# The dense attention's keys and values move into seven-product pairs, and its conditioning is summed in wider pieces

## The chip, the cores and the metric

The kernel runs on one core of one Trainium2 chip. The metric is the device time of one execution, in microseconds (us), as the median of several runs. One more execution was recorded by the hardware profiler; all views of the profile below come from that one.

## The reference

One inference step of a trunk with two layers, for 512 latent tokens and 128 context tokens (640 columns in all, width 2048). Every layer does the same: RMS norm of x with a scale and a shift that come from a conditioning vector, one input projection whose columns feed two mixers and their gates, one output projection, and a gated residual. The conditioning of a layer is `silu(cond) @ ada_w[layer] + ada_b[layer]`, 6144 columns for each of two vectors.

The second ("odd") layer is the one that the change touches:

```
cq, ck, cv, cg, dq, dk, dv, dg = split_cols(h @ w_in, ODD_SPLIT)   # 1024,1024,1024,1024,1024,256,256,1024
o_c = rms_norm(o1 - lam * o2, c_on) * (1 - lam_init)               # mixer C: two softmax maps for each of 4 heads
y_d = merge_heads(attend(q_d, dk_all, dv_all)) * silu(dg)          # mixer D: 8 query heads, 2 key/value heads
x   = x + gate * (concatenate([y_c, y_d]) @ w_out)
```

Mixer D is dense attention: queries and keys are normed and turned by a rotary table, the latent tokens attend to 256 cached context tokens and all 512 latents, the context tokens only to themselves. Its two key heads and two value heads are 128 columns each, so each is one tile of the projection. The new keys and values of the context tokens are outputs as well.

## The kernel before

All activations lie transposed: 16 tiles of 128 channels by 640 tokens. A projection **tile** is 128 output channels: 16 blocks of weights, each held as a high and a low part (`split`, L295, one ACT copy and one DVE subtraction, L296 and L297), times the activations, held in the same way. Three products (high x high, high x low, low x high) and two halves of 320 tokens make 96 matmuls of 128x320 in `proj_q` (L324, L331 to L333). A **quarter** of a tile is four blocks, 24 matmuls.

Where several tiles need only be projected, two are taken together as a **pair** in `run_pairs` (L523): a two by two scheme of seven products of half the size instead of eight. Each product is 8 blocks x 3 = 24 matmuls of 128x320 (L616 to L618); the combined weights are summed on DVE (L555 to L567), the combined activations (`forms`, L1137) were made once. After each of the seven products (M1, M5, M6, M2, M7, M3, M4) `after` copies or adds its result (L588 copies that of M1).

The second layer has three stages.

- **The front** (`project`, called at L1671 with `run_pairs` behind it) projects 14 of the 16 gate tiles and the eight value tiles of mixer C, 22 tiles: the first `N_FRONT = 6` singly, the other 16 as eight pairs. `front_begin` (L1652) chooses what becomes of each tile. A gate (`gate_out`) is stored to a scratch tensor in DRAM; a value (`value_out`, `value_rows`) is copied to SBUF, transposed to token rows by PE, copied by ACT and stored to the scratch `vdram` and, for the context tokens, to the output, both on POOL's DMA queue.
- **The odd stage** (`run_tiles` with the list `jobs`, L1689 to L1710) projects the remaining tiles singly and works the attention in between. Its 28 jobs are, for each half of mixer D, `dq0 dq1 dk dv dq2 dq3`, and then, for each head of mixer C, `cq cq ck ck`; two late gates follow. The function of a finished tile (`q_gen` L727, `k_gen` L660, `v_gen` L774) is a generator, put on the list `prep`.
- **The output projection** (`project_out`, called at the end).

What sets the order: the code issues a quarter of a tile and then calls `slot` (L371). A slot takes every generator of `prep` one step on, takes the attention list `attn` on by `steps` steps (1.0 by default; `brisk` gives 1.1 from job 13 on and 1.5 for the last two jobs), and takes the fill on by `rate` steps (`FILL1 = 1.3`, from the ninth slot on). All of `prep` is drained before the next tile's generator begins. Attention generators (`pair_gen` L858 for two heads of mixer D, `diff_gen` for mixer C) make about two steps for each block of 128 queries, one for each score. `k_gen` and `v_gen` call `drain(attn)` before they write the tiles that the attention reads, so that a second key or value first forces out all attention that is still waiting; `q_gen` does so while as many attentions wait as there are sets of query tiles (two). A score takes the only PSUM buffer of the name `S` (L826), and gives it back when the exponential (L800) has read it. From this list the compiler makes each engine's own order, which need not be the code's.

A weight quarter is loaded on SP's queue up to five quarters ahead into four buffers (`RAW_AHEAD`, `load_raw`, L309) and split three ahead (`SPLIT_AHEAD`).

The fill is `ada_on_dve` (L191): the last four 512-column blocks of the layer's conditioning. Each block is summed over 16 row blocks on DVE, for two conditioning vectors, in two parts of 256 columns; `scalar_tensor_tensor` (L218) multiplies by the vector's element and adds. The weights come on SP's queue (L206, tile `adaw`, three buffers) one step ahead. A copy from the last weight split (`mark`) keeps a block from starting before its place.

## Time and profile before

| | us |
|---|---|
| median of 3 runs | 2280.9 |
| lowest and highest run | 2277.78 and 2281.18 |
| the profiled execution | 2276.21 |
| its span, from the first to the last instruction | 2274.3 |

The granted TensorE clock was 0.997 of full speed on average. In the views, PE is the matmul engine, PEld its weight loading, DVE, ACT and POOL the three others, and SP the engine that issues most loads. A name such as `pa<-h,wh` gives the tile written and the tiles read; L331 is a line of the kernel before. Matmuls overlap each other, so their mean duration (some 310 ns) is longer than the distance from one to the next, and idle time of PE counts only what no matmul covers.

### The profile page before, as it was taken

The page shows a single profiled execution, that of the slowest core. Times are in us where ns is not written, and L with a number is a line of the kernel's source. Part 1 is how long each engine was busy: PE and PEld are TensorE (multiplying, and loading weights), DVE is VectorE, ACT ScalarE, POOL GpSimd, SP SyncE. Part 2 cuts the span into 40 slices and gives each one's busy share as a digit, 9 for nine tenths or more (in the row PEclk, how much of TensorE's full clock was granted, in tenths as well). Part 3 has the DMA queues.
Part 4 walks back from the last instruction along what each step waited for, and adds up shares of the span by engine and source line. Part 5 has one row for each costly group of instructions (what it writes and reads, how often), then busy time and mean ns, then how long its engine had stood idle before and what let it go on. Part 6 is the DMA issues. An engine that isn't in the chain of part 4 may idle for free.

```text
span 2274.3 us, 41403 instructions
## 1 busy us (share of the span) xinstructions
PE 2237.6 (98%) x15760; PEld 2155.6 (95%) x15760; DVE 1680.4 (74%) x3133; ACT 1113.0 (49%) x2293; POOL 207.9 (9%) x305
## 2 busy tenths in 40 slices
PE   8999999999999999999999999999999999999999
PEld 5889999999799999999999999999999999999999
DVE  5659889987857778887876754857758788677665
ACT  4336554544334445444744455566665455554343
POOL 2220000000000000000200000010010211211010
PEclk9999999999999999999999999999999999999999
DMA  9984556564833326643763334423324234237541
GB/s 358 344 292 145 175 172 202 168 186 148 261 102 99 91 91 225 212 141 112 250 213 109 114 109 135 132 70 96 100 75 147 89 107 126 89 119 241 152 135 49
DMA packets 387400, 351.45 MB, mean 155 GB/s; under 512 B 17906, under 2 KB 341968, under 8 KB 386688
## 3 DMA queue, kind: packets, MB, share of 16 engines
q1 hardware_dynamic: 373360, 298.15, 42.9%
q0 software_dynamic: 12976, 48.41, 5.8%
q8 instruction: 124, 2.03, 0.4%
q10 hardware_dynamic: 864, 2.23, 0.3%
q14 instruction: 76, 0.62, 0.1%
HBM read 305.86 MB, written 42.86 MB: 153 GB/s over the span
## 4 chain that ended last, share of the span: by engine, by line
PE 84%; DVE 5%; DMA 4%; ACT 3%; issue 2%; POOL 1%; SPq 0%; DVEq 0%; ACTq 0%; POOLq 0%
PE pq L617 10%; PE pq L618 10%; PE pq L616 10%; PE pa L331 7%; PE pb L331 6%; PE pb L332 6%; PE pa L332 6%; PE pb L333 6%; PE pa L333 6%; PE T L819 2%; PE S L831 1%; DMA adaw<-in_ada_w 1%; PE S L833 1%; PE S L832 1%; PE T L646 1%
## 5 line engine op out<-in xcount | busy, mean ns | idle before, releaser
L296 ACT ACTIVATE wh<-raw 128x512 fp32r<-128x512 f32 (+1 forms) x400 | 241.2, 604 | 412.3 <-PE pb L332 289.4
L331 PE MATMUL pa<-h,wh 128*128 128x320 f32 x1216 | 389.4, 320 | 0.5 <-DVE sum L420 0.5
L332 PE MATMUL pa<-h,wh 128*128 128x320 f32 x1216 | 378.5, 311 | 0.9 <-DVE h L297 0.9
L331 PE MATMUL pb<-h,wh 128*128 128x320 f32 x1216 | 378.2, 312 | 0.9 <-ACT h L296 0.9
L333 PE MATMUL pb<-h,wl 128*128 128x320 f32 x1216 | 377.8, 311 | 0.0
L332 PE MATMUL pb<-h,wh 128*128 128x320 f32 x1216 | 377.7, 311 | 0.0
L333 PE MATMUL pa<-h,wl 128*128 128x320 f32 x1216 | 377.3, 310 | 0.0
L297 DVE TENSOR_TENSOR wl<-raw,wh 128x512 fp32r<-128x512 f32 (+1 forms) x400 | 262.1, 656 | 151.1 <-ACT wh L296 138.2
L616 PE MATMUL pq<-h,wh 128*128 128x320 f32 x896 | 277.2, 309 | 0.0
L618 PE MATMUL pq<-h,wl 128*128 128x320 f32 x896 | 276.9, 309 | 0.0
L617 PE MATMUL pq<-h,wh 128*128 128x320 f32 x896 | 276.8, 309 | 0.0
L331 PEld LDWEIGHTS pa<-h,wh 128*128 128x128 f32 x1216 | 228.8, 188 | 16.1 <-issue 11.0
L332 PEld LDWEIGHTS pa<-h,wh 128*128 128x128 f32 x1216 | 229.0, 188 | 7.3 <-issue 6.2
L331 PEld LDWEIGHTS pb<-h,wh 128*128 128x128 f32 x1216 | 229.4, 189 | 2.9 <-issue 1.2
L332 PEld LDWEIGHTS pb<-h,wh 128*128 128x128 f32 x1216 | 229.3, 189 | 1.3 <-issue 1.2
L333 PEld LDWEIGHTS pa<-h,wl 128*128 128x128 f32 x1216 | 228.4, 188 | 2.1 <-issue 2.1
L333 PEld LDWEIGHTS pb<-h,wl 128*128 128x128 f32 x1216 | 229.3, 189 | 0.4 <-issue 0.4
L616 PE MATMUL pq<-T,wh 128*128 128x320 f32 x672 | 208.0, 309 | 0.0
L617 PE MATMUL pq<-T,wh 128*128 128x320 f32 x672 | 207.6, 309 | 0.0
L618 PE MATMUL pq<-T,wl 128*128 128x320 f32 x672 | 207.3, 308 | 0.0
L258 DVE SCALAR_TENSOR_TENSOR acc<-adaw,sT,acc 128x1024 f32<-128x1024 f32 x150 | 189.5, 1280 | 0.0
L296 ACT ACTIVATE wh<-sx 128x512 fp32r<-128x512 f32 x168 | 105.6, 633 | 147.5 <-PE pq L617 101.0
(379 smaller groups left out, 4634.5 us busy)
## 6 DMA issues: line engine op xcount, KB each, us to landing
adaw<-in_ada_w SPq DMA_DIRECT2D x80, 512.0 KB, 3.9
raw<-in_od_w_in SPq DMA_DIRECT2D x160, 256.0 KB, 2.9
raw<-in_ev_w_in SPq DMA_DIRECT2D x130, 256.0 KB, 3.4
ada<-in_ada_w SPq DMA_DIRECT2D x11, 2048.0 KB, 13.8
adaw<-in_ada_w SPq DMA_DIRECT2D x128, 128.0 KB, 2.2
w<-in_ev_w_in SPq DMA_DIRECT2D x27, 512.0 KB, 3.7
w<-in_od_w_in SPq DMA_DIRECT2D x24, 512.0 KB, 3.8
adah<-in_ada_w SPq DMA_DIRECT2D x20, 512.0 KB, 9.5
```

The costliest lines, as they stand in the source:

```text
L258: V.scalar_tensor_tensor(out=acc[c], in0=w, scalar=sT[:, kt, c:c + 1], in1=acc[c], op0=ALU.mult, op1=ALU.add)
L296: A.activation(hi, x, AF.Copy)
L297: V.tensor_sub(lo, x, hi)
L331: PE.matmul(ps, wh[:, i, :], hi[:, sl], start=(j == js[0] if alone else (pos == 0 and j == 0)), stop=False)
L332: PE.matmul(ps, wh[:, i, :], lo[:, sl], start=False, stop=False)
L333: PE.matmul(ps, wl[:, i, :], hi[:, sl], start=False, stop=(j == js[1] - 1 if alone else (pos == 3 and j == 3)))
L616: PE.matmul(ps, wh[:, j, :], hi, start=(first and h == 0 and j == 0), stop=False, skip_group_check=True)
L617: PE.matmul(ps, wh[:, j, :], lo, start=False, stop=False, skip_group_check=True)
L618: PE.matmul(ps, wl[:, j, :], hi, start=False, stop=(final and h == 1 and j == 3), skip_group_check=True)
L646: PE.transpose(t[:, i * P:(i + 1) * P], src(b), ident)
L819: PE.transpose(t[:, i * P:(i + 1) * P], p, ident)
L831: PE.matmul(d, q[0][:, bs], k[0][:, ks], start=True, stop=False)
```

## The change

The two key tiles and the two value tiles of mixer D leave the list of jobs and join the front's list, as two more pairs between the gates and the values of mixer C. The front has 26 tiles and ten pairs, the odd stage 24 jobs and the two late gates.

A key is copied to SBUF by `key_out` and stored to a new scratch tensor `kdram`. At the start of the odd stage `keys_first` loads both, and `k_gen` works them one after the other, two steps in each slot (`in_twos`). A value goes the way of mixer C's values, with two more places of `vdram`; its rows come back in `with_values`, a first step ahead of the attention of each half's first pair of heads, which also splits them and the cached values.

The fill sums 512 columns at a time: half as many loads, twice as large, two buffers for three. `FILL1` becomes 0.85. `brisk` gives 1.5 attention steps a slot for jobs 2 to 9 and 1.1 from job 10 on. Three small things make room in SBUF: two unused results (`junk`) are written as bf16, and `le` shares the tile of `ls`.

```diff
-FILL1 = 1.3
+FILL1 = 0.85
...
+    def ada_on_dve(blocks):
...
+            acc = [ap.tile([P, 512], F32, tag=f"acc{c}", name=f"acc{c}", bufs=1) for c in range(2)]
+            for c in range(2):
+                V.tensor_copy(acc[c][:, 0:1], mark[0])
+            def fetch(kt):
+                w = ap.tile([P, 512], F32, tag="adaw", name="adaw", bufs=2)
+                nc.sync.dma_start(w, I["ada_w"][l, kt * P:(kt + 1) * P, cb * 512:(cb + 1) * 512])
+                return w
+            nxt = fetch(0)
+            for kt in range(KT):
+                w, nxt = nxt, (fetch(kt + 1) if kt + 1 < KT else None)
                 for c in range(2):
...
+                        V.scalar_tensor_tensor(out=acc[c], in0=w, scalar=sT[:, kt, c:c + 1], in1=acc[c],
                                                op0=ALU.mult, op1=ALU.add)
                 yield
...
-        x = stage(ap, pp)
+        if isinstance(pp, tuple):
+            x = stage(ap, pp)
+        else:
+            x = ap.tile([P, NT], F32, tag="stg", name="kx", bufs=2)
+            nc.sync.dma_start(x, pp)
...
+    def with_values(values, ap, width, k, *rest):
+        rows_, src = values
+        raw = ap.tile([P, 5, P], F32, tag="ctxv", name="vrow", bufs=1)
+        ctx_ = ap.tile([P, 2, P], F32, tag="ctxk", name="vctx", bufs=1)
+        nc.sync.dma_start(raw.rearrange("p b f -> p (b f)"), rows_)
+        nc.sync.dma_start(ctx_, src.rearrange("(c p) d -> p c d", p=P))
+        yield
+        hi, lo = st["v"] = tuple(ap.tile([P, 7, P], F32R, tag=t, name=t) for t in ("vh", "vl"))
+        split(hi[:, 2:7, :], lo[:, 2:7, :], raw)
+        split(hi[:, 0:2, :], lo[:, 0:2, :], ctx_)
+        yield from pair_gen(ap, width, k, st["v"], *rest)
...
-        nc.gpsimd.dma_start(O["new_c_v"][0, 0, n // 2][:, n % 2 * P:(n % 2 + 1) * P], r[:, 4, :])
+        nc.gpsimd.dma_start(O["new_c_v"][0, 0, n // 2][:, n % 2 * P:(n % 2 + 1) * P] if n < 8
+                            else O["new_d_v"][0, 0, n - 8], r[:, 4, :])
...
+    def key_out(j):
+        x = xr_tile("kx")
+        def put(t, sl, src):
+            A.copy(x[:, sl], src)
+            if (j, "k") in half_done:
+                nc.gpsimd.dma_start(kdram[j], x)
+            half_done.add((j, "k"))
+        return put
...
-            + [OD["cv"] + i * P for i in range(8)], N_FRONT, h1_maker,
+            + [OD[n] + i * P for n, m in (("dk", 2), ("dv", 2), ("cv", 8)) for i in range(m)], N_FRONT, h1_maker,
...
-        then = pair_then(768, f"k{kv}", 8 + h, False, gated)
+        then = pair_then(768, f"k{kv}", 8 + h, False, gated,
+                         (vdram[8 + kv], I["cache_d_v"][0, 0, kv]) if n % 2 == 0 else None)
         jobs.append((OD["dq"] + h * P, q_job("q0", "d_q_norm")))
-        jobs.append((OD["dq"] + (h + 1) * P, q_job("q1", "d_q_norm", then if n % 2 else None)))
-        if n % 2 == 0:
-            jobs.append((OD["dk"] + kv * P, k_job(f"k{kv}", I["cache_d_k"][0, 0, kv], "d_k_norm", O["new_d_k"][0, 0, kv])))
-            jobs.append((OD["dv"] + kv * P, v_job(I["cache_d_v"][0, 0, kv], O["new_d_v"][0, 0, kv], then)))
+        jobs.append((OD["dq"] + (h + 1) * P, q_job("q1", "d_q_norm", then)))
+    def keys_first():
+        for kv in range(2):
+            yield from k_job(f"k{kv}", I["cache_d_k"][0, 0, kv], "d_k_norm", O["new_d_k"][0, 0, kv])(kdram[kv])
+    def in_twos(g):
+        while next(g, DONE) is not DONE and next(g, DONE) is not DONE:
+            yield
+    prep.append(in_twos(keys_first()))
...
-    brisk.update((i, 1.1) for i in range(13, len(jobs)))
+    brisk.update((i, 1.5 if i < 10 else 1.1) for i in range(2, len(jobs)))
```

More of the change, by code (lines that the diff above doesn't have):

```diff
@@ L675, in k_gen @@
         kg = ap.tile([P, 5, P], F32, tag="rp", name="kg", bufs=3)
-        junk = ap.tile([P, P * st["sets"]], F32, tag="junk", name="junk", bufs=1)[:, 0:P]
+        junk = ap.tile([P, P * st["sets"]], BF16, tag="junk", name="junk", bufs=1)[:, 0:P]
         for sample in (True, False):
@@ L932, in trunk_kernel @@
     fill0b = ada_beside([(1, 2), (1, 3)])
-    fill1 = ada_on_dve([(1, cb) for cb in range(8, 12)], ("acc0", "acc1", "adaw", "adaw", "adaw", "adaw"), 2,
-                       lambda: mark[-1])
+    fill1 = ada_on_dve([(1, cb) for cb in range(8, 12)])
     ydram = [dram.tile([P, NT], F32, name=f"yd{k}") for k in range(KT)]
     x0dram = [dram.tile([P, 4 * NT + 1], F32, name=f"x0d{g}") for g in range(4)]
+    kdram = [dram.tile([P, NT], F32, name=f"kd{k}") for k in range(2)]
     xdram, hdram, gdram, vdram = ([dram.tile([P, NT], F32, name=f"{n}{k}") for k in range(KT)]
@@ L1057, in gate_job, with pair_then @@
         return f
-    def pair_then(width, kk, i, banded, gated):
+    def pair_then(width, kk, i, banded, gated, values=None):
         def then():
@@ L1516, in odd_start @@
         V.tensor_reduce(ls, lp, axis=AX.X, op=ALU.add)
-        le = small.tile([P, 2], F32, tag="le", name="le", bufs=1)
+        le = ls
         A.activation(le, ls, AF.Exp)
@@ L1577, in weigh @@
             ssq = small.tile([P, 1], F32, tag="ssq", name="ssq")
-            junk = ap.tile([P, 256], F32, tag="junk", name="junk")
+            junk = ap.tile([P, 256], BF16, tag="junk", name="junk")
             A.activation(junk, on, AF.Square, accum_out=ssq)
@@ L1654, in front_begin @@
             n = N_FRONT + 2 * p + t
[L1655 removed]
+            m = n - len(FRONT)
+            outs[t] = gate_out(n) if m < 0 else key_out(m) if m < 2 else value_out((m - 4) if m > 3 else m + 6)
     def front_done(p, t, h, src):
```

25 lines of the change are left out of this document (4 added, 21 removed).

## The prediction, made before the result

> **What bounds the kernel now.** I read the page first (busy shares and the chain of work that ended last), then windows by stage, then the waits of the engine that the chain names.
>
> ```profile
> span 2274.3 us, 41403 instructions
> PE 2237.6 (98%) x15760; PEld 2155.6 (95%) x15760; DVE 1680.4 (74%) x3133; ACT 1113.0 (49%) x2293; POOL 207.9 (9%) x305
> PE 84%; DVE 5%; DMA 4%; ACT 3%; issue 2%; POOL 1%; SPq 0%; DVEq 0%; ACTq 0%; POOLq 0%
> ```
>
> TensorE (PE) holds 98% of the span and 84% of the chain; no other engine comes near. A change pays if it takes matmuls away from PE without opening new idle time on it. The windows (microseconds; busy time and instruction count of PE, PEld, DVE, ACT, POOL, then the granted clock) show where PE is idle. 1127 to 1191 is the end of the front's six single tiles, up to 1389 run its eight pairs, then the second layer's attention stage ("odd") until about 2062.
>
> ```profile
> 1127.00:1191.00 64.00, 64.00 (x438) 64.00 (x438) 51.83 (x93) 31.97 (x57) 5.40 (x10) 1.00 0.69 212
> 1191.00:1245.00 54.00, 54.00 (x370) 54.00 (x369) 37.74 (x57) 25.27 (x47) 2.16 (x4) 1.00 0.39 119
> 1396.00:1456.00 60.00, 59.07 (x409) 57.56 (x408) 41.75 (x93) 25.89 (x60) 5.97 (x5) 1.00 0.51 155
> 1456.00:1576.00 120.00, 119.89 (x858) 115.89 (x856) 77.17 (x171) 79.85 (x161) 8.79 (x9) 1.00 0.26 78
> 1576.00:1636.00 60.00, 57.68 (x405) 55.85 (x404) 49.12 (x112) 34.08 (x67) 4.55 (x6) 1.00 0.39 119
> 1636.00:1696.00 60.00, 59.90 (x427) 57.72 (x426) 31.94 (x67) 41.35 (x84) 5.18 (x5) 1.00 0.22 67
> 1756.00:2062.00 306.00, 300.45 (x2103) 288.51 (x2101) 229.58 (x509) 161.13 (x396) 47.33 (x72) 1.00 0.35 107
> ```
>
> The front has no idle PE time at all: 438 matmuls in 64 us and 370 in 54 us, 146 ns each. The dense attention (1456 to 1756) has almost none either, except 2.3 us in 1576 to 1636, where the second key and value tiles pass. So the end moves with the number of matmuls, and what PE's waits become decides the rest.
>
> ```profile
> PE S L831 <- ACT p L800: 1.4, 3, 0.8
> PE T L882 <- DVE y L1072: 1.2, 1, 1.2
> PE T L646 <- DVE k0l L297: 0.9, 1, 0.9
> PE S L831 <- ACT p L800: 1.1, 2, 0.8
> ```
>
> The first three are PE's waits over the whole odd stage, the last those of 1576 to 1612 alone (total, times, longest). The y wait of 1.2 and the score wait of 1.1 are the 2.3 us of the second key and value tiles; the k0l wait of 0.9 is the first key's.
>
> **The change part by part.** *Four tiles become two pairs.* A single tile is 16 weight blocks x 3 products x 2 halves = 96 matmuls, two are 192; a pair is 7 products x 8 blocks x 3 = 168. The period of a pair is read from the copy after its first product, four gate pairs and then four value pairs:
>
> ```profile
> L588 ACT COPY tables<-pq x4: 408/409/411, 1196.0 to 1269.8; 128x320 f32<-128x320 f32 x4
> L588 ACT COPY tables<-pq x4: 407/408/409, 1294.5 to 1371.6; 128x320 f32<-128x320 f32 x4
> ```
>
> A gate pair lasts (1269.8 - 1196.0) / 3 = 24.6 us; two single tiles last 192 x 146 ns = 28.0. That is 3.4 us a pair, **-6.8 us** for two. A value pair lasts 25.7: the 1.1 more are the ten transposes of its rows, which the value tiles of the odd stage run today and the front takes over, so nothing is gained or lost. The keys' transposes stay in the odd stage.
>
> [...]
>
> *What moves with them.* To the front: four half copies for the keys, four for the values, two row copies each for the values on ACT, and two stores of keys, two of values and two outputs on POOL's queue. ACT is busy 25.3 of 54 us there and POOL 2.2, PE waits for neither; if that cover were gone, the copies at 0.41 us each would be exposed after each product. Out of the odd stage go 16 weight splits, eight staging copies and the two vp copies with their output stores; SP's weight loads only change place. Into it come four loads on SP's queue (two keys, two value rows). The value rows are split by ACT at the head of an attention step, behind which scores' exponentials and weight splits queue; the load is issued one step ahead, and I cost it at nothing. `le = ls` and the bf16 junk tiles change no count of instructions; I cost them at nothing.
>
> *The keys at the start.* Both keys are now prepared during job 0, two steps per quarter. The first wait of 0.9 us (k0l) stays, in another place; the second key's tail comes right behind it with the same chain: **+0.9**. Gone is what k1 and v1 did in the middle, with their forced draining of the attention: **-2.3**. New is that PE transposes a tile just loaded. Nearest rows:
>
> ```profile
> y<-gd SPq DMA_DIRECT2D x14, 320.0 KB, 3.8
> 1398.27 0.38 SPq L309 DMA_DIRECT2D raw<-in_od_w_in  x1
> ctxk<-in_cache_c_k SPq DMA_DIRECT2D x8, 128.0 KB, 2.4
> ctxk<-in_cache_d_k SPq DMA_DIRECT2D x2, 128.0 KB, 3.4
> 1389.11 0.30 PE L331 MATMUL pb<-h,wh 128*128 128x320 f32 x1
> 1390.21 0.77 PE L646 MATMUL T<-ident,acc 128*128 128x128 f32 x5
> ```
>
> The same 320 KB from a scratch tensor land 3.8 us after issue, and SP is through the first loads about 9 us after job 0 starts, while a job lasts 14 us. So between 0 and +3.8 us. The last two rows show that PE's order is not the code's: job 0's matmuls run ahead of transposes that the code issues before them, so projection fills such holes. In the odd stage no PE wait of the trace is on a DMA, though ten context-key loads feed transposes there. I take **0**. Behind the transposes stands the projection of job 0; q0's staging shares the two `stg` buffers with the keys and would hold ACT by as much.
>
> *The sums of the conditioning.*
>
> ```profile
> L218 DVE SCALAR_TENSOR_TENSOR acc<-adaw,sT,acc x240: 465/480/489, 1421.5 to 1913.1; 128x256 f32<-128x256 f32 x120
> L216 DVE TENSOR_SCALAR acc<-adaw,sT x16: 334/349/353, 1421.0 to 1881.4; 128x256 f32<-128x256 f32 x16
> L1013 DVE SCALAR_TENSOR_TENSOR ht<-xT,gsc,tables 128x512 f32<-128x512 f32 x16 | 12.0, 749 | 1.2 <-ACT tables L990 0.9
> SPq L206 <- DVE acc L218: 72.5, 74, 4.1
> ```
>
> Today 240 x 480 + 16 x 349 = 121 us of DVE; at 512 columns 120 x 749 plus 8 at some 480 (an estimate, between the 349 and twice it) = 94. DVE loses 27 us of work, PE nothing, for PE waits nowhere in the odd stage on these sums. Half as many loads, twice as large, with two buffers for three: SP waits on the sums already (72.5 us), in turn with the weight loads behind it; a weight part is split three quarters ahead, 3 x 3.5 us, which covers it. Cost 0; without that cover, at most the longest such wait, 4.1 us, once a block.
>
> *The attention gets denser.* This is the price. Today an attention step goes with each quarter of a tile (24 matmuls, 3.5 us); afterwards 1.5 steps do, in jobs 2 to 9.
>
> ```profile
> L793 DVE TENSOR_REDUCE nm<-S 128x1 f32<-128x768 f32 (+1 forms) x19 | 16.1, 847 | 2.5 <-PE S L833 2.4
> L331 PE MATMUL pa<-h,wh 128*128 128x320 f32 x83 | 27.0, 325 | 0.0
> L331 PE MATMUL pb<-h,wh 128*128 128x320 f32 x80 | 24.7, 309 | 0.0
> L793 DVE TENSOR_REDUCE nm<-S 128x1 f32<-128x768 f32 x7 | 6.7, 954 | 1.7 <-PE S L833 1.7
> L793 DVE TENSOR_REDUCE nm<-S 128x1 f32<-128x128 f32 x2 | 0.6, 284 | 0.0
> PE T L819 <- DVE p L1555: 0.6, 1, 0.6
> PE T L1591 <- DVE ptl L297: 0.9, 2, 0.5
> ```
>
> The first three rows are 1456 to 1576: 19 steps (one maximum each) in 120 us, 6.3 us a step, of which 3 x 163 x 146 ns / 19 = 3.8 are projection and 2.5 attention and queries. Afterwards a step has 3.5 / 1.5 = 2.3 us of projection: 4.9 us. ACT's 79.85 us and DVE's 77.17, less some seven weight splits, are then 4.0 and 3.8 us a step, 80% of the time where they are 65% now. The last four rows are 2008 to 2050, where the last tiles already run at 1.5 steps: 9 steps in 42 us, 4.7 us apart, and PE waits 0.6 us for a probability tile, and 0.9 for outputs normed in a way that the dense steps don't have. That is 0.07 us a step, 0.17 with both, against 0 at 6.3 us. Four pairs have 40 such steps. Bounds 0 and 40 x 0.17 = 6.7; between the rows at 4.7 and 6.3, 4.9 us gives 0.06: **+2.4**.
>
> Sum: -6.8 - 2.3 + 0.9 + 0 + 0 + 2.4 = **-5.8 us**. The profiled execution took 2276.2 us, 1.9 of it outside the span; it would take 2270.4. The median of the runs shown is 2280.9, 4.7 above the profiled one, and the same step gives **2275.1**. A measurement of this kernel can tell 0.2%, 4.6 us, from no change.
>
> **The rivals.** *The gain is eaten.* The dense steps pay the full late price, 6.7, and nothing else changes: -1.5 us, **2279.4**; with the keys' load exposed as well, 3.8, it is 2283.2. For it: ACT and DVE both near 80%. Against it: 1636 to 1696 has ACT at 41 of 60 us with 0.1 us of PE idle. One more thing could add to it.
>
> ```profile
> 1060.00:1127.00 67.00, 63.29 (x418) 62.41 (x417) 51.08 (x99) 41.29 (x82) 10.52 (x18) 0.95 0.65 213
> ```
>
> Where PE idled 3.7 us, before the front, the granted clock fell to 0.95 over 67 us, 3.4 us of work; the odd stage with its short waits has 1.00 throughout. Keys that land late in one piece could buy the same again. [...]
>
> *Slower: the single score bank becomes the bound.* A score needs the exponential before it to have left `S`. Where DVE also sums the conditioning, two scores follow like this:
>
> ```profile
> 1600.40 0.44 PE L831 MATMUL S<-k1h,q1h 128*128 128x384 f32 x1 [0.29 <-ACT p L800]
> 1605.99 0.44 PE L831 MATMUL S<-k1h,q0h 128*128 128x384 f32 x1 [0.77 <-ACT p L800]
> ```
>
> The cycle is 5.6 us, 0.7 over the 4.9 to come. In half of the 40 steps that costs 14 us in place of 2.4: -8.2 + 14 = +5.8, **2286.7**. It eats the gain from 12 steps on and is slower by 0.2% from 19. For it: the sums come in dense bursts (DVE 49 of 60 us in 1576 to 1636). Against: at 4.7 us spacing in 2008 to 2050 no score waited.
>
> *A larger gain.* With 27 us less on DVE, the 5.6 us that PE idles in 1756 to 2062 halve and the dense steps wait for nothing: -6.8 - 2.3 + 0.9 - 2.8 = -11.0, **2269.9**. Against it: that stage's waits are mostly on POOL's and ACT's results, not on the sums.
>
> **How the numbers follow.** Forecast 0.48 (its own range 2272 to 2278), gain eaten 0.27, score bank 0.15, larger gain 0.10. Faster by over 0.2%: 0.42 of the forecast and the 0.10, 0.52. Slower: 0.15 and 0.03 of the eaten case, 0.18. Within: the rest, 0.30. The range runs from 2268, below the larger gain, to 2286, past the eaten case at its worst (2283.2) and almost to the score bank's; some 0.14 is left out.
>
> **What would show it.** Ten pair periods of 24.6 to 25.8 us in the front with PE fully busy, and an odd stage that starts 50 us later and is about 56 us shorter. No y wait of 1.2 us in the middle of the dense heads. Steps 4.9 us apart there, with PE idle of 2 to 3 us in all; 7 or more would mean the gain is eaten, and `S` waits of 0.7 us each the score bank. A PE wait on a key's load at the start, or a granted clock under 1.00, would make the 0 wrong. DVE's sums should fall from 121 to about 94 us.

## The result, and the profile after

The changed kernel took 2286.99 us (median of 8 runs, 2282.26 to 2289.99), the kernel before beside it 2280.45 (8 runs): a ratio of **1.0028**, 95% interval 1.0019 to 1.0038, 6.4 us slower (the two medians lie 6.5 apart). The forecast was 5.8 us faster. The profiled execution took 2286.38 us.

First the page of the kernel after.

```profile
span 2284.5 us, 41077 instructions
PE 2238.1 (98%) x15712; PEld 2151.5 (94%) x15712; DVE 1682.6 (74%) x3029; ACT 1123.8 (49%) x2313; POOL 207.7 (9%) x309
PE 83%; ACT 5%; DMA 4%; DVE 4%; issue 3%; POOL 1%; SPq 0%; ACTq 0%; DVEq 0%; POOLq 0%
```

PE's records fell from 15760 to 15712 and still its busy time is the same (2237.6 before). PE remains the bound; ACT's share of the chain rose from 3% to 5%. Next the copy behind each pair's first product, of the four gate pairs ahead of the keys and of the six pairs from the keys on, as one row each; then DVE's sums and the maxima of the dense heads (minimum, median and maximum in ns, first and last start).

```profile
L581 ACT COPY tables<-pq x4: 407/407/408, 1200.7 to 1274.6; 128x320 f32<-128x320 f32 x4
L581 ACT COPY tables<-pq x6: 407/408/408, 1299.2 to 1426.7; 128x320 f32<-128x320 f32 x6
L211 DVE SCALAR_TENSOR_TENSOR acc<-adaw,sT,acc x120: 725/743/753, 1485.3 to 1917.2; 128x512 f32<-128x512 f32 x120
L209 DVE TENSOR_SCALAR acc<-adaw,sT x8: 476/480/486, 1484.5 to 1860.9; 128x512 f32<-128x512 f32 x8
L790 DVE TENSOR_REDUCE nm<-S x40: 277/953/959, 1491.6 to 1708.5; 128x1 f32<-128x768 f32 x32, 128x1 f32<-128x128 f32 x8
```

There are ten pairs, the first copy at 1200.7 and the last at 1426.7, 226.0 us for 175.6 before: 50.4 longer, as forecast. (1274.6 - 1200.7) / 3 = 24.6 us a gate pair; the six later ones last 25.5 on average. The sums take 120 x 743 + 8 x 480 ns = 93 us. So the front and the work of the sums came out as worked out (DVE's total did not fall, 1682.6 us for 1680.4; two more pairs bring sums of their own); the loss stands behind them. One part of it is no effect of the change: of the 10.2 us between the two profiled spans, 4.7 are there before the first pair (its first copy starts at 1196.0 and at 1200.7), in stages that the change leaves alone. In the other profiles this copy starts between 1196 and 1202 whichever list of tiles the kernel has, but for the three whose query copies were moved. The odd stage in three windows, up to the first score, the dense heads (mixer D), and mixer C with the late gates up to the output projection, first of before, then of after:

```profile
1389.80:1454.00 64.20, 63.27 (x438) 61.59 (x437) 41.14 (x91) 26.45 (x63) 7.04 (x7) 1.00 0.54 164
1454.00:1722.00 268.00, 265.45 (x1892) 256.36 (x1890) 179.38 (x404) 172.21 (x348) 20.72 (x22) 1.00 0.29 89
1722.00:2145.00 423.00, 412.56 (x2862) 398.72 (x2862) 312.37 (x671) 208.78 (x491) 59.74 (x92) 1.00 0.43 134
```

```profile
1444.90:1490.00 45.10, 42.02 (x279) 39.31 (x278) 26.52 (x54) 24.17 (x65) 6.75 (x9) 0.96 0.53 168
1490.00:1729.00 239.00, 235.23 (x1661) 223.66 (x1660) 168.84 (x338) 162.96 (x322) 19.26 (x17) 1.00 0.33 98
1729.00:2155.00 426.00, 411.27 (x2858) 396.49 (x2857) 308.93 (x624) 207.63 (x488) 58.18 (x92) 1.00 0.44 134
```

The first number behind the length is PE's busy time, so PE idles 0.9, 2.6 and 10.4 us before and 3.1, 3.8 and 14.7 after. The stage was to become some 56 us shorter; the three lengths became 755.2 - 710.1 = 45.1 shorter. What left the stage is 57.2 us of PE's work, 384 matmuls of 146 ns and ten transposes (1.1 us), so 12.1 us are lost. 7.7 of them are new idle time. PE's busy time fell by only 52.8, so 4.4 more are lost in what counts as busy. Pauses that an overlapping matmul covers are not counted as idle; whether the 4.4 us lie there is not shown. Two things are to be seen. The largest new idle time, 4.3 us, stands in mixer C, whose tiles the change does not touch. And in the first window the granted clock is 0.96. The kernel before has such a stretch too, in its third window (0.59 from 2125.0 to 2129.2), where the changed one has none, so between these two executions the clock of the stage makes no difference. The first window's waits, then those of the dense heads, then mixer C's (total, times, longest):

```profile
PE T L639 <- DMA kx<-kd: 1.9, 1, 1.9
PE T L639 <- DVE kg L689: 1.1, 2, 0.9
...
PE S L828 <- ACT p L797: 3.0, 7, 0.7
...
PE T L816 <- DVE p L1565: 3.5, 4, 2.3
PE S L828 <- ACT p L797: 2.9, 4, 1.6
PE T L639 <- DVE k0l L290: 2.8, 2, 1.7
```

Before, mixer C had 1.2 us of probability waits and 0.4 of score waits. The timeline shows the late key and what it set off, on SP's queue and then on PE:

```profile
1441.80 8.48 SPq L302 DMA_DIRECT2D raw<-in_od_w_in  x4
...
1451.87 0.89 SPq L667 DMA_DIRECT2D kx<-kd  x2
...
1457.19 0.81 PE L639 MATMUL T<-ident,kx 128*128 128x128 f32 x3 [1.86 <-DMA kx<-kd]
```

```profile
1450.40:1453.80 3.40, 3.40 (x25) 3.40 (x24) 0.69 (x1) 0.63 (x1) 0.00 (x0) 1.00 0.62 174
1453.80:1457.20 3.40, 1.54 (x12) 1.31 (x10) 1.28 (x5) 0.20 (x1) 0.00 (x0) 1.00 0.98 319
1457.20:1460.60 3.40, 3.40 (x14) 3.40 (x15) 0.79 (x2) 2.09 (x10) 0.00 (x0) 0.51 0.71 268
```

SP's first row joins four weight loads of some 0.37 us each. What fills the 8.48 us is SP's wait for the weight buffers, which the splits on DVE free (total, times, longest, in 1440 to 1452):

```profile
SPq L302 <- DVE wl L290: 8.0, 4, 3.7
```

The kernel before has the same four loads and the same 8.0 us of waiting. In the changed one the keys' loads stand behind them in the queue, and PE waited 1.86 us. In the 3.4 us behind that wait PE started 14 matmuls where 25 had fitted, at a clock of 0.51: another 1.7 us. And the 2.3 us wait in mixer C, on DVE and POOL:

```profile
2064.00 0.82 DVE L290 TENSOR_TENSOR h<-yin,h 128x640 fp32r<-128x640 f32 x1 [0.40 <-ACT h L289]
2065.55 0.48 DVE L1596 SCALAR_TENSOR_TENSOR on<-on,rn,con 128x256 f32<-128x256 f32 x1 [0.73 <-POOL rn L1592]
2065.96 0.35 DVE L1565 SCALAR_TENSOR_TENSOR p<-p,w 128x128 f32<-128x128 f32 x1
...
2066.45 0.30 PE L816 MATMUL T<-ident,p 128*128 128x128 f32 x1 [2.32 <-DVE p L1565]
```

The probability stood in DVE's queue behind an output's norm, which waited for POOL, and behind a split for the output projection. None of these instructions is new: it is old work met in another order.

### The profile page after: what moved, and what is told of

Same layout as the page of the kernel before. It is cut to its first block, busy times and chain, and to the rows that moved or that the text cites. A ratio compares the mean times of both kernels' runs of the same rounds, so it can differ in the third digit from the quotient of the medians.

```text
span 2284.5 us, 41077 instructions
## 1 busy us (share of the span) xinstructions
PE 2238.1 (98%) x15712; PEld 2151.5 (94%) x15712; DVE 1682.6 (74%) x3029; ACT 1123.8 (49%) x2313; POOL 207.7 (9%) x309
## 4 chain that ended last, share of the span: by engine, by line
PE 83%; ACT 5%; DMA 4%; DVE 4%; issue 3%; POOL 1%; SPq 0%; ACTq 0%; DVEq 0%; POOLq 0%
PE pq L609 11%; PE pq L611 11%; PE pq L610 11%; PE pa L324 6%; PE pa L325 6%; PE pb L324 6%; PE pb L325 6%; PE pa L326 6%; PE pb L326 6%; PE T L816 2%; PE S L828 1%; PE S L830 1%; PE S L829 1%; PE T L178 1%; PE T L639 1%
## 5 line engine op out<-in xcount | busy, mean ns | idle before, releaser
L324 PE MATMUL pa<-h,wh 128*128 128x320 f32 x1152 | 369.3, 321 | 0.3 <-DVE sum L413 0.3
L325 PE MATMUL pa<-h,wh 128*128 128x320 f32 x1152 | 360.0, 313 | 1.4 <-DVE h L290 1.4
L324 PE MATMUL pb<-h,wh 128*128 128x320 f32 x1152 | 358.3, 312 | 0.9 <-ACT h L289 0.9
L326 PE MATMUL pa<-h,wl 128*128 128x320 f32 x1152 | 359.1, 312 | 0.0
L326 PE MATMUL pb<-h,wl 128*128 128x320 f32 x1152 | 358.4, 311 | 0.0
L325 PE MATMUL pb<-h,wh 128*128 128x320 f32 x1152 | 358.0, 311 | 0.0
L609 PE MATMUL pq<-h,wh 128*128 128x320 f32 x960 | 297.5, 310 | 0.0
L610 PE MATMUL pq<-h,wh 128*128 128x320 f32 x960 | 296.6, 309 | 0.0
L611 PE MATMUL pq<-h,wl 128*128 128x320 f32 x960 | 296.3, 309 | 0.0
L324 PEld LDWEIGHTS pa<-h,wh 128*128 128x128 f32 x1152 | 217.7, 189 | 15.5 <-issue 10.4
L325 PEld LDWEIGHTS pa<-h,wh 128*128 128x128 f32 x1152 | 217.8, 189 | 8.1 <-issue 6.2
L609 PE MATMUL pq<-T,wh 128*128 128x320 f32 x720 | 223.3, 310 | 0.0
L611 PE MATMUL pq<-T,wl 128*128 128x320 f32 x720 | 222.5, 309 | 0.0
L610 PE MATMUL pq<-T,wh 128*128 128x320 f32 x720 | 222.4, 309 | 0.0
L324 PEld LDWEIGHTS pb<-h,wh 128*128 128x128 f32 x1152 | 217.2, 189 | 2.9 <-issue 1.3
L325 PEld LDWEIGHTS pb<-h,wh 128*128 128x128 f32 x1152 | 217.3, 189 | 0.8 <-issue 0.8
```

Source lines behind the costliest of these rows:

```text
L324: PE.matmul(ps, wh[:, i, :], hi[:, sl], start=(j == js[0] if alone else (pos == 0 and j == 0)), stop=False)
L325: PE.matmul(ps, wh[:, i, :], lo[:, sl], start=False, stop=False)
L326: PE.matmul(ps, wl[:, i, :], hi[:, sl], start=False, stop=(j == js[1] - 1 if alone else (pos == 3 and j == 3)))
L609: PE.matmul(ps, wh[:, j, :], hi, start=(first and h == 0 and j == 0), stop=False, skip_group_check=True)
L610: PE.matmul(ps, wh[:, j, :], lo, start=False, stop=False, skip_group_check=True)
L611: PE.matmul(ps, wl[:, j, :], hi, start=False, stop=(final and h == 1 and j == 3), skip_group_check=True)
```

## The experiments

Times are medians; ratios are to the kernel before, run beside each on the same chip. 0.001 is 2.3 us. Idle times are those of the three windows above, at each kernel's own edges.

| kernel | us | ratio | idle: start, dense, mixer C |
|---|---|---|---|
| the change | 2286.99 | 1.0028 [1.0019, 1.0038] | 3.1, 3.8, 14.7 |
| e1 before, wide sums | 2284.02 | 1.0015 [1.0003, 1.0028] | 1.7, 4.0, 11.9 |
| e2 change, narrow sums | 2282.76 | 1.0012 [1.0001, 1.0024] | 3.4, 4.0, 12.5 |
| e3 change, keys loaded first | 2285.84 | 1.0025 [1.0016, 1.0034] | 3.9, 3.2, 15.4 |
| e4 values only | 2279.67 | 0.9994 [0.9983, 1.0005] | 0.5, 4.6, 9.5 |
| e5 change, keys in job 1 | 2282.63 | 1.0033 [1.0020, 1.0047] | 2.1, 3.8, 14.9 |
| e6 the same, narrow sums | 2280.68 | 1.0015 [1.0004, 1.0025] | 2.1, 3.6, 12.3 |
| e7 change, no sums | 2278.82 | 1.0006 [0.9997, 1.0015] | 3.8, 4.2, 10.9 |
| e8 before, no sums | 2270.09 | 0.9971 [0.9959, 0.9982] | 0.0, 0.3, 9.9 |
| e9 before, dense pace | 2284.76 | 1.0023 [1.0012, 1.0033] | 0.7, 3.5, 9.0 |
| e10 change, no maximum | 2287.84 | 1.0030 [1.0018, 1.0042] | 3.3, 3.9, 13.8 |
| e11 before, no maximum | 2277.43 | 0.9987 [0.9976, 0.9998] | 1.2, 1.9, 9.7 |
| e12 change, slower pace | 2286.90 | 1.0033 [1.0020, 1.0045] | 3.0, 5.0, 14.2 |
| e13 keys only | 2286.45 | 1.0024 [1.0015, 1.0033] | 4.1, 3.8, 10.6 |
| e14 change, swap on GpSimd | 2310.83 | 1.0130 [1.0114, 1.0147] | 3.2, 7.6, 18.4 |
| e15 before, swap on GpSimd | 2301.64 | 1.0094 [1.0078, 1.0110] | 1.8, 3.2, 12.6 |
| e16 values only, swap on GpSimd | 2303.61 | 1.0099 [1.0085, 1.0113] | 1.3, 7.8, 14.2 |
| e17 values only, key ahead | 2280.31 | 0.9998 [0.9988, 1.0008] | 1.1, 2.4, 12.5 |
| e18 change, narrow sums, old pace | 2279.03 | 0.9991 [0.9982, 1.0000] | 4.0, 3.1, 10.8 |

**The width of the sums (e1, e2).** e1 puts the change's `ada_on_dve` into the kernel before (with the two bf16 junk tiles, which make room), e2 puts the old one back into the change.

```diff
-FILL1 = 1.3          (e1, from before)
+FILL1 = 0.67
...
-FILL1 = 0.85         (e2, from the change)
+FILL1 = 1.65
...
```

> The kernel before with one part of the change alone: the conditioning summed 512 columns at a time (two buffers, rate 0.67, so that the blocks are spread over as many slots as before) and the bf16 junk tiles. Theory A (the loss of some 11 us in the odd stage comes from the keys' late loads at its start and from the denser attention; the width of the sums does not matter): the same as before, within 2 us, and PE's idle time in the odd stage near 10 us. Rival B (sums of 743 ns in place of 480 stand longer ahead of the short instructions of the softmax on DVE, and that is what PE waits for): 4 us slower than before or more, with the score waits (S on ACT p) up from 1.4 us to 4 or more.

> The changed kernel with the sums of before: 256 columns, three buffers, rate 1.65 so that the blocks end at the same slot. Theory A: as the changed kernel, 1.0028 of before within 0.1%, score waits near 5.9 us. Rival B: back to before or faster, 2281 us or less, score waits under 3 us.

Fewer, longer sums cost time, though they take 28 us less of DVE: +3.4 us alone, and their removal from the change gives 3.7 back. Both lie between the two expectations, nearer to rival B. In e1's dense heads the score waits rise to 2.6 us, from the 1.1 that the prediction's row for the second keys shows:

```profile
PE S L824 <- ACT p L793: 2.6, 2, 1.6
```

The longer of these two waits ends at 1609.10. DVE's rows ahead of it:

```profile
1606.11 0.95 DVE L786 TENSOR_REDUCE nm<-S 128x1 f32<-128x768 f32 x1
1606.98 0.74 DVE L211 SCALAR_TENSOR_TENSOR acc<-adaw,sT,acc 128x512 f32<-128x512 f32 x1
1607.64 0.21 DVE L788 TENSOR_SCALAR nm<-nm,rq 128x1 f32<-128x1 f32 x1
```

A sum stands between the maximum and its scaling, and the exponential that frees the score buffer starts behind the scaling, at 1607.96. The longest score wait of the changed kernel (1.6 us, in mixer C) has a sum in the same place, and e2 has no score wait over 0.5 us left in mixer C. In the changed kernel's dense heads sums are the smaller part: of the seven score waits one has a sum between maximum and scaling, the six others a product of the next query's rotation, of 0.68 us (L735). The width came together with loads twice as large and two buffers for three; no run separates these.

**The keys' place (e3, e5, e6).** e3 issues the keys' loads before job 0's work, e5 starts the keys in job 1, e6 does so with narrow sums.

```diff
-    prep.append(in_twos(keys_first()))
+    keys = keys_first()                       (e3)
+    next(keys)
+    prep.append(in_twos(keys))
...
+    def with_keys(fn):                        (e5, e6)
+        def run(g):
+            for i, _ in enumerate(g):
+                if i == 0:
+                    prep.append(in_twos(keys_first()))
+                yield
+        return lambda pp: run(fn(pp))
+    jobs[0] = jobs[0][0], with_keys(jobs[0][1])
```

> The changed kernel with one edit: the generator of the keys takes its first step before the weight loads of the odd stage are issued, so that the first key's load stands ahead of four weight loads on SP's queue in the code. Theory A: the wait of 1.9 us for the loaded key goes, and with it the 3.4 us of halved clock behind it (1.7 us of work); 2 to 4 us faster than the changed kernel, 1.001 to 1.002 of before. Rival B: as the changed kernel.

> The changed kernel with the two keys worked in the slots of job 1 instead of job 0, so that their loads have a whole tile (14 us) more to land. If the late key costs what the trace shows (1.9 us of waiting, some 0.9 for the second key's tail, and in some runs a stretch of halved clock): 2 to 4 us faster than the changed kernel, 1.001 to 1.002 of before, no PE wait on the load. If it costs nothing beyond what projection fills: as the changed kernel, 1.0025 to 1.003.

> The changed kernel with both edits: sums of 256 columns at rate 1.65, and the keys in job 1. If the two costs are separate and add up (4 us for the wide sums, 2 to 4 for the keys): 2279 to 2281 us, as before or a little faster, 0.999 to 1.0005. If the denser attention alone still costs more than the pairs bring: slower than before, 1.001 or more.

e3 told nothing: the compiler gave SP and PE the same order as in the changed kernel, and PE waited for the load as before (1.9 us). It is a second measurement of the change. In e5 the wait for the load is gone (0.2 us in its trace) and the time is not better, 1.0033 for 1.0028; e6 against e2 says the same. PE idles 2.1 us before the first score where the change has 3.1, and the rest of the stage is as it was; why the runs are no faster is not shown. e6 against e5 is a third measurement of the sums' width: 0.0018 or 4.1 us.

**Without the sums (e7, e8).** Both leave out the four conditioning blocks; the gate is a constant.

```diff
-    fill1 = ada_on_dve([(1, cb) for cb in range(8, 12)])        (e7; e8 likewise)
+    fill1 = iter(())
+    V.memset(hgt[1], 0.5)
```

> The changed kernel without the four conditioning blocks that are summed in the odd stage: the gate of the second layer's residual is a constant instead. It leaves out some 94 us of work on DVE and 64 loads. If the sums are what makes the denser attention wait: score waits under 2 us (5.9 in the changed kernel) and 5 us or more faster than the next run, the kernel before without its sums. If the density alone makes PE wait: score waits stay at 4 us or more, and it is no more than 3 us faster than the next run.

> The kernel before without its four conditioning blocks, as the run above: the yardstick for it. Either theory: 1 to 4 us faster than the kernel before (some of its 9.6 us of PE idle time in the odd stage goes), score waits under 1.4 us.

The sums are not free in either kernel: they cost the kernel before 6.6 us and the changed one 5.0. But without them the change is still 0.0035 or 8.0 us behind. Neither expectation of e7 had that: its score waits stay at 4.8 us, as density alone would have it, but it was then to be at most 3 us behind e8; and e8 gained 6.6 where 1 to 4 were expected. The windows up to the first score and of the dense heads, e8 and then e7:

```profile
1393.00:1456.00 63.00, 63.00 (x436) 61.35 (x435) 23.55 (x43) 26.27 (x62) 6.29 (x7) 1.00 0.40 117
1456.00:1719.00 263.00, 262.66 (x1871) 255.36 (x1870) 142.00 (x294) 171.01 (x346) 20.55 (x21) 1.00 0.22 66
```

```profile
1441.00:1486.00 45.00, 41.24 (x276) 38.97 (x276) 24.18 (x47) 23.52 (x63) 6.43 (x9) 0.96 0.47 149
1486.00:1722.00 236.00, 231.78 (x1638) 221.85 (x1637) 131.50 (x271) 159.78 (x312) 18.92 (x17) 1.00 0.21 64
```

With the sums away, the kernel before idles 0.3 us in these two windows, the changed one 8.0, and 0.96 is again the clock of the first. That is what the new place of the keys and values and the density cost with no sum on DVE; 3.9 us of e7's idle time in the dense heads are score waits. The costs do not add up: with narrow sums in both kernels the change is 2.7 us behind (e2), with none 8.0, so the same narrow sums cost the kernel before 6.6 us and the changed one some 1.3.

**One pair alone (e4, e13).** e4 moves only the value pair, e13 only the key pair; both have narrow sums and 1.25 steps a slot in jobs 3 to 9.

```diff
...
+            + [OD[n] + i * P for n, m in (("dv", 2), ("cv", 8)) for i in range(m)]    (e4)
+            + [OD[n] + i * P for n, m in (("dk", 2), ("cv", 8)) for i in range(m)]    (e13)
...
+    brisk.update((i, 1.25 if i < 10 else 1.1) for i in range(3, len(jobs)))
```

> The kernel before with the two value tiles alone moved to the front as a ninth pair; the keys stay tiles of the odd stage, the sums stay at 256 columns, and the dense attention goes at 1.25 steps a slot in jobs 3 to 9. Theory A: 3.4 us less for the pair, no late key, the density paid in part (some 2 us): 1 to 3 us faster than before. Rival B: the full 3.4 us faster, since the sums are narrow. A third reading, that a pair more in the front does not pay at all there: same as before or slower, with a pair period over 25.8 us.

> The kernel before with only the key pair moved to the front and both keys worked at the start of the odd stage; the values stay single tiles there, the sums stay 256 columns wide, 1.25 attention steps a slot in jobs 3 to 9. One pair is worth -3.4 us. Theory (the keys' new place at the start costs about 5 us: two key chains in a row, behind a load that TensorE waits for 2 us, and then often 3.4 us at half clock): 2281 to 2284 us, and TensorE idles 3 us or more before the first score. Rival (the loss belongs to the density that both pairs make): like the values alone, 2278 to 2280.5 us.

The values alone are even with the kernel before (-1.4 us, interval -3.9 to 1.1), the keys alone lose 5.5, above the range that was expected. Together that is 4.1, and e2, both pairs with narrow sums, has 2.7. So the keys are the pair that does not pay: both versions have the same pace and the same narrow sums, and lie 6.9 us apart. e13's first window and its waits:

```profile
1416.00:1472.00 56.00, 51.88 (x356) 48.69 (x355) 35.75 (x77) 26.21 (x71) 8.43 (x10) 1.00 0.55 163
```

```profile
PE T L646 <- DVE kg L696: 1.8, 2, 1.0
PE T L646 <- DMA kx<-kd: 1.8, 1, 1.8
PE T L755 <- ACT qs L750: 0.4, 1, 0.4
```

PE idles 4.1 us there, 0.9 before. This profile is of the fastest of e13's 11 runs (2278.54 us, clock 0.998; no half clock behind the wait); most of the others have a clock of 0.994 to 0.996.

**The pace (e9, e12).** e9 gives the kernel before 1.5 steps a slot in jobs 4 to 12, e12 gives the change 1.25 for 1.5.

```diff
-    brisk.update((i, 1.1) for i in range(13, len(jobs)))
+    brisk.update((i, 1.1 if i > 12 else 1.5) for i in range(4, len(jobs)))          (e9)
-    brisk.update((i, 1.5 if i < 10 else 1.1) for i in range(2, len(jobs)))
+    brisk.update((i, 1.25 if i < 10 else 1.1) for i in range(2, len(jobs)))         (e12)
```

> The kernel before with 1.5 attention steps a slot in jobs 4 to 12 in place of 1.0; tiles, pairs, sums and loads stay. Theory (density: two scores close behind each other wait for the exponential to free the only score buffer): score waits of TensorE in the odd stage rise from 1.4 us to 4 us or more, its idle time there from 9.6 us by 3 to 5, and the kernel takes 2283 to 2286 us. Rival (the loss comes with the tiles that left the stage, not with the pace): score waits stay under 2.5 us and the kernel within 1.5 us of the one before, 2279 to 2282.

> The changed kernel with 1.25 attention steps a slot in jobs 2 to 9 in place of 1.5: the same tiles and steps, 5.7 us apart for 4.9, the rest forced out when the next queries need their places. Theory (score buffer): steps are further apart, score waits fall from 9 us to 5 or less, and the kernel takes 2282 to 2285 us, 2 to 4 us less than the changed one. Rival (the work is what it is, and what is forced out at the end of a pair of heads costs what the even pace saved): 2286 us or more.

e9 is inconclusive. Its median lies where the theory had it, but its trace is of the fastest of 11 runs (2278.44) and has 0.4 us of score waits, so it does not show the mechanism. What the runs say is that this pace alone makes the kernel before 5.2 us slower. e12 went against the theory: the score waits fell to 4.7 us as expected, but its transposed probabilities waited in their place, and the time stayed.

**The maximum left out (e10, e11).** Both leave out mixer D's row maximum and the scale of its scores, so that the exponential follows the scores directly.

```diff
-        V.tensor_reduce(nm, s, axis=AX.X, op=ALU.max, negate=True)
+        if not flat:
+            V.tensor_reduce(nm, s, axis=AX.X, op=ALU.max, negate=True)
...
-        A.activation(p[:, 0:n], s, AF.Exp, scale=rsc, bias=nm, accum_out=l)
+        A.activation(p[:, 0:n], s, AF.Exp, scale=peps if flat else rsc, bias=nm, accum_out=l)
```

> The changed kernel with mixer D's row maximum and the scale of its scores left out: the exponential follows the scores directly, so the score buffer is held about 1 us less (0.83 us of reduction and one small operation), and DVE has some 37 us less work. Theory (score buffer): score waits fall from 9 us to 3 or less, idle time of TensorE in the odd stage from 17 us to 10 or less, and the kernel takes 2278 to 2281 us, while the kernel before with the same cut gains 2 us at most. Rival (other engines being fuller, whatever the buffer): score waits fall but idle time stays over 13 us, since transposes and projections then wait, and the kernel takes 2283 us or more.

> The kernel before with mixer D's row maximum and the scale of its scores left out, the control of the same cut in the changed kernel. Theory (score buffer is what the changed kernel pays for): it had 1.4 us of score waits to lose, so 2278 to 2280.5 us, and the distance between the two kernels shrinks from 6.5 us to 2 or less. Rival (DVE's load as such): both gain alike, the distance stays at 5 us or more.

My theory of the score buffer fell here. e10's dense heads:

```profile
1488.00:1729.00 241.00, 237.11 (x1671) 225.41 (x1670) 134.66 (x260) 163.41 (x322) 20.56 (x19) 1.00 0.33 99
```

```profile
PE S L831 <- ACT p L800: 1.3, 1, 1.3
PE T L882 <- ACT pth L289: 1.3, 3, 0.7
PE T L883 <- DVE ptl L290: 0.8, 2, 0.4
```

Score waits fell from 3.0 to 1.3 us, DVE from 169 to 135, and PE idles 3.9 us, as with the maximum: waits for the split probabilities took the place. The time did not move, while the control gained 3.0. So the buffer is where the wait shows, not what decides it.

**ScalarE relieved (e14, e15, e16).** The four part copies of a query go from ScalarE to GpSimd, in the change, in the kernel before and in e4.

```diff
-            A.copy(sw[32 * d:32 * d + 32, :], x[32 * (d ^ 1):32 * (d ^ 1) + 32, 0:NS])
+            nc.gpsimd.tensor_copy(sw[32 * d:32 * d + 32, :], x[32 * (d ^ 1):32 * (d ^ 1) + 32, 0:NS])
```

> The changed kernel with the four part copies of each query (0.62 us each, 32 of them in the dense heads, 19.8 us) issued on GpSimd in place of ScalarE. Theory (ScalarE's queue is what the dense heads wait for: the exponential that frees the score buffer and the split of the transposed probabilities stand in it behind those copies): TensorE's idle time in the dense heads falls from 3.75 us to 2 or less, and the kernel takes 2281 to 2284 us, 3 to 5 less than the changed kernel, while the kernel before with the same edit gains at most 2. Rival (whatever is taken off one engine, the next wait takes its place, as with the maximum left out): idle time there stays at 3 us or more, and the kernel takes 2285 us or more.

> The kernel before with the four part copies of each query on GpSimd in place of ScalarE, the control of the same edit in the changed kernel. Theory (ScalarE's queue decides only where the steps are dense): 2278.5 to 2281 us. Rival (both gain alike, the edit has nothing to do with the density): 2276 to 2278 us.

> The kernel with only the value pair in the front (narrow sums, keys as before) and the four part copies of each query on GpSimd in place of ScalarE, a version that could beat both kernels. Theory (ScalarE's queue holds the score buffer, which costs this version 4.9 us of score waits): 2274 to 2277.5 us, faster than both. Rival (no gain from ScalarE's relief): 2278.5 to 2281 us.

All three became 21 to 30 us slower, the control too; it tells little of the density. A copy takes 772 ns on GpSimd where it took 618 on ScalarE, every query of both layers has four, and the query's chain follows them:

```profile
L732 POOL COPY qsw<-qx 32x512 f32<-32x512 f32 x32 | 24.7, 772 | 89.5 <-ACT qx L728 74.1 <-issue 14.4
```

In e14 the odd stage already starts 15 us later. Whether ScalarE's queue bounds the dense heads stays open.

**Two last ones (e17, e18).** e17 is e4 with the key ahead of its half's second query and the old pace in mixer C's first job. e18 is e2 with the old pace from the first job of mixer C on.

```diff
...
+        if n % 2 == 0:                                                              (e17)
+            jobs.append((OD["dk"] + kv * P, k_job(...)))
         jobs.append((OD["dq"] + (h + 1) * P, q_job("q1", "d_q_norm", then)))
...
-    brisk.update((i, 1.5 if i < 10 else 1.1) for i in range(2, len(jobs)))          (e18)
+    brisk.update((i, 1.5 if i < 8 else 1.1) for i in range(2, len(jobs)) if i != 8)
```

> The kernel with only the value pair in the front, and each key's single tile now ahead of the second query of its half instead of behind it, so that a tile of projection lies between the key's chain and the first score; one attention step a slot in the first job of mixer C, as the kernel before has it there. A version that could beat both. Theory (the tiles that left were what covered the key's chain: with cover back, its waits go): of the 4.6 us that TensorE idles in the dense heads with the values alone (2.0 of them on the second key, with 1.7 lost at half clock behind it) 2.5 or less are left, and the kernel takes 2274 to 2277.5 us. Rival (another wait takes their place): 4 us or more are left there, 2278.5 to 2281 us.

> The changed kernel with 256-column sums and, from the last two queries of mixer D on, exactly the pace of the kernel before (one step a slot in the first job of mixer C, 1.1 from the second on, where the change has 1.5 in both). Mixer C's tiles are the same in all kernels, so what it loses there can only come from how its steps fall against its tiles. Theory (alignment): TensorE's idle time from mixer C's start to the output projection falls from 12.5 us to the 10.4 of the kernel before, and the kernel takes 2279 to 2281.5 us. Rival (mixer C loses by something else that comes with the change): it stays at 12 us or more and the kernel at 2282 us or more.

e18 tests mixer C. Its last window, then e2's, and e18's waits there:

```profile
1728.00:2153.00 425.00, 414.18 (x2867) 398.73 (x2865) 317.93 (x691) 208.25 (x490) 60.68 (x93) 1.00 0.45 137
```

```profile
1726.00:2149.00 423.00, 410.48 (x2857) 396.13 (x2856) 317.28 (x688) 207.40 (x491) 59.37 (x92) 1.00 0.44 135
```

```profile
PE T L823 <- DVE p L1573: 1.7, 4, 0.5
...
PE S L835 <- ACT p L804: 0.3, 1, 0.3
```

PE's idle time there is 10.8 us, 12.5 in e2 and 10.4 before; the 2.3 us probability wait is gone, and the score waits are those of before. The ratio goes from 1.0012 to 0.9991 (each against the kernel before on its own chip): 4.8 us for two jobs' pace, uncertain by some 3.3. The traces show less, 1.7 us of idle time in mixer C and 0.9 in the dense heads, and e18's is of the slowest of its 12 runs. The two jobs are also not mixer C's alone: by the count of their matmuls they run from about 1616 to 1672 in the changed kernel, under the last dense heads. Nor is the pace a rule for mixer C: e9 has 1.5 steps in its first job and idles only 9.0 us there. In e17, which has the old pace in that job, the dense heads did what was expected (2.4 us idle for 4.6), but mixer C took 12.5 for 9.5, and the time stayed. Its dense heads, then e4's:

```profile
1477.00:1723.00 246.00, 243.56 (x1723) 232.70 (x1722) 172.30 (x384) 166.21 (x336) 19.51 (x19) 1.00 0.30 89
```

```profile
1482.00:1726.00 244.00, 239.37 (x1686) 229.46 (x1685) 167.46 (x370) 163.89 (x329) 20.01 (x20) 0.99 0.29 87
```

No version beat the kernel before by what can be measured; e18, the best that computes all, is 2.1 us faster, interval 0 to 4.1.

## Why the prediction was wrong

Forecast and measurement lie 12.2 us apart (-5.8 and +6.4). Point by point, by its own steps:

- **Two pairs, -6.8: right.** Four gate pairs of 24.6 us, six further pairs of 25.5 on average, and a front 50.4 us longer. This gain was really made.
- **The waits in the middle, -2.3: right.** The 1.2 us y wait is gone, and no key or value chain stands in the dense heads' waits.
- **The density, +2.4: near in idle time, not settled in cost.** The dense heads idle 3.8 us in the change and 3.1 in e18, where the 2.6 of before, less the 2.3 of the middle, plus 2.4 was expected. But the pace alone made the kernel before 5.2 us slower (e9). DVE and ACT came to 71% and 68% of the time there, not to 80%. The steps are further apart than the 4.9 us forecast: (1708.5 - 1491.6) / 39 = 5.6 on average, gaps between the pairs of heads included. Score waits of 0.7 us at half of all 40 did not come; there are 3.0 us of them in all, and 3.9 in e7, which has no sums.
- **The sums, "cost 0": wrong, 3.7 us** (e2 against the change; alone 3.4, e1; 4.1 between e5 and e6). The step said that PE waits nowhere on these sums. That is true of the rows and no reason: PE waits for results that stand behind a sum in DVE's queue, as e1's rows show, and what counts there is, as far as e1 and e2 separate it, the length of one sum, 743 ns for 480, not their total. e8 shows that even the old sums, which no row named, cost 6.6 us.
- **The keys at the start, +0.9 and 0: wrong, by 1.3 to 3 us in the trace and more by the runs.** Idle time up to the first score rose by 2.2 us where 0.9 was forecast; 1.7 more went to the half clock behind it, which the kernel before lost elsewhere in its stage. By the runs the keys' move is 6.9 us dearer than the values' (e13 and e4), waits in the middle included. The bound for the load, 3.8, and the danger of the clock stood in the text; I took the lower end because projections had filled such holes. They did not here: four weight loads, each waiting for its buffer, went ahead of the keys on SP, and PE had nothing to fill 1.86 us with.
- **What was not in the sum at all: mixer C.** It idles 4.3 us more than before, and no term of the sum looked past the dense heads. I read the pace of 1.5 in "jobs 2 to 9" as the dense heads' alone. Jobs 8 and 9 already project mixer C's first two tiles; the extra steps move every later step against its tile, and with it which work meets in DVE's queue. With narrow sums 2.2 of the 4.3 us go (e2), with the old pace 1.7 more (e18). By the runs the pace is worth 4.8 us, uncertain by 3.3.

One after the other, e2 and e18 take 3.7 and 4.8 us from the change and leave it 2.1 us faster than the kernel before, where 5.8 was forecast. The 3.7 us that are then left fit the keys' 3 and the half microsecond of the dense heads. That this closes is luck: each step is uncertain by some 3 us, and the terms depend on each other, as the 8.0 us without sums against the 2.7 with narrow ones show.

Of the rivals, the gain was eaten, and by more than its worst case, because that case had only the dense heads and the load. The slower rival gave 2286.7, close to the 2286.99 measured, by luck and for the wrong reason: it wanted 14 us of score waits in the dense heads, and there are 3.0. These waits are real, but e10 took 1 us from each cycle of the buffer and gained nothing.

What stays open: why e9 is 5.2 us slower, which its trace does not show; where the 4.4 us went that the changed kernel's odd stage loses in busy time; and which queue decides the waits of the dense heads, since taking away the maximum (e10) and a slower pace (e12) only let another wait show.

## What to carry to other kernels

An engine off the critical path is to be judged by the instruction that can stand ahead of a short one that the critical engine awaits, and not by its total alone (in e1, sums of 743 ns for 480, 28 us less of DVE in all, and 3.4 us slower). A step that is moved keeps its own chain but loses the work that covered it, and a pace that is counted through moves everything behind it, so its price has to be looked for in stages that the diff does not name. Where two engines are some 70% busy, as DVE and ACT in these dense heads, taking one wait away mostly showed the next (e10, e12).

## What the runs showed of the hardware

Behind a single wait of 1.86 us the changed kernel's trace shows half clock. In the 3.41 us before the half clock (1453.86 to 1457.27) PE was busy for 1.55 us, then 3.41 us went at 0.50. It is no rule: of nine profiles with this wait for a key's load (1.8 to 2.5 us), seven have the half clock behind it, and the granted clock of their first window is 0.96 or 0.97. In e13, where the wait is 1.8 us, that window has 1.00, and e3, with 1.9 us, has no half clock there either. So such a wait cost 1.7 us more, as in the changed kernel's trace, or nothing; what decides between the two is not shown.

The granted clock also orders the runs of one and the same kernel. The kernel before, 35 runs beside e1 to e4:

| granted clock | runs | mean us |
|---|---|---|
| 0.998 | 8 | 2277.4 |
| 0.997 | 15 | 2280.6 |
| 0.996 | 6 | 2281.8 |
| 0.995 | 6 | 2284.0 |

That is 2.2 us for 0.001, as much as 0.1% of the span. The mean clock was 0.9967 in these runs, 0.9961 in the eight of the changed kernel and 0.9964 in the twelve of e3, which has the same order: of the 6.4 us some one, an estimate from this table, came through the clock. A change that adds such a wait can pay for it twice, the second time only in some executions, here in seven of the nine profiled.
